# Layer 1's windowed attention on one Trainium2 core: when the exponentials, the division and the gates' loads of a unit are issued

## The chip, the cores and the metric

The kernel runs on one core of one Trainium2 chip. The metric is the device time in microseconds (us) of one launch, median of the runs. Five engines of the core appear in the profile: TensorE (PE, with its weight loads as PEld), VectorE (DVE), ScalarE (ACT), GpSimd (POOL), and SyncE (SP), on whose queue all of this kernel's loads and stores are issued.

## What is computed

One inference step of a two-layer encoder over 2048 prompt frames and 64 sample frames, 1024 wide, in float32. Layer 0 mixes two attentions; the change lies in layer 1, whose attention reads a window of three chunks of 64 frames (its own and two before), with 16 query heads, 2 key heads and a learned sink per head, and whose output is gated and projected:

```python
def _c_layer(h, pos, cache, pre_g, post_g, w_in, sinks, w_out):
    xn = _rms(h, pre_g)
    q, k, v, g = _split(xn @ w_in, C_SIZES)
    ...
    o = _band_prompt(q, k, v, C_PAST_CHUNKS, C_SCALE, sinks=sinks)
    ...
    return h + _rms((o * jax.nn.silu(g)) @ w_out, post_g), state

    s = jnp.einsum('...qhgd,...khd->...hgqk', q, k).astype(jnp.float32) * scale
    s = jnp.where(valid, s, NEG_INF)
    sk = jnp.broadcast_to(sinks.astype(jnp.float32).reshape(hk, g, 1, 1), s.shape[:-1] + (1,))
    p = jax.nn.softmax(jnp.concatenate([s, sk], axis=-1), axis=-1)[..., :-1]
    return jnp.einsum('...hgqk,...khd->...qhgd', p.astype(v.dtype), v)
```

## The kernel before

The kernel runs in five phases. Phase 4 computes layer 1's queries, keys, values and gates (`sQC`, `sKC`, `sVC`, `sGC` in memory), and phase 5, with which the change deals, does layer 1's attention and output projection together. Numbers are kept as a rounded high part and a low part, so that a product of two such numbers is three matmuls (a "triple").

The 2048 frames are 16 blocks of 128, taken in the order 8 to 15, then 0 to 7. A block is four units: chunk `ch` 0 or 1, key head `g` 0 or 1, in the order (0,0), (0,1), (1,0), (1,1). `class Unit` has the stages of a unit:

- `start` (`score`, L1697 to L1701): 8 matmuls give the scores s, 128 rows by 4 x 192 columns; DVE takes the maxima (L1699) and two small results in m (L1700, L1701).
- `exp` (L1708, L1711): ACT computes four exponentials of 128x192 into P, with their sums, and one of the sinks.
- `divide` (L1715 to L1717): DVE adds the sink's term to the sums, takes reciprocals, and multiplies P by them.
- `turn` (L1723): PE transposes P for one part of the window (128 keys, or 64) into t; ACT copies it to PT's high half (L211), and `low` has DVE form the low half (L214).
- `av` (L1730): four matmuls with the values into acc.
- `out` (L1814): ACT copies half of acc to tbm (L211), and DVE adds the halves into the block's output tile OT. After the last unit of a block, the generator `gate` is put into `J.side`.

`gate` loads the gates G (L1735), pauses, multiplies OT by G on POOL (L1738), waits until fewer than two blocks stand between it and the projection, then splits the product into MM: the high half on ACT (L211), the low half on POOL (L1745). The projection multiplies MM by W_out (L964, 16 triples a block); its result z goes through ACT (copy, squares L983), small operations of the inverse root on POOL and DVE (L987, L186 to L197), two multiplications on DVE (L995), and the addition of the residual x on POOL (L1003), and is stored (L1006).

`step(n)` issues one step of a pipeline over the units: the exponentials of unit n+1, the score of unit n+2, unit n's two transposes with `pump(2)` behind each (two triples of the projection), unit n-1's `av` and `out` between them, and at the end unit n+1's division. `J.rest` then moves the gate's generator and the projection's tail by one pause each. The first 8 steps are put in order by a scheduler; for the other 57 the order of PE, DVE, ACT and SP is the order in which the code issues (`manual`), while POOL's is the scheduler's. Every engine takes its instructions in order. OT has two buffers, P three, s two, and G two. A block that would open a third OT (`J.open >= 2`) issues extra `J.rest` and one triple at a time until an older OT is done.

Of the kernel before, what the change touches and what calls it, by code (L numbers as in the profile page):

```python
# [7 lines left out]
F32 = mybir.dt.float32  # L8
# [8 lines left out]
SEQ, DS, PAST, DM = 2048, 64, 1024, 1024  # L17
# [93 lines left out]
def kernel(ctx, tc, a, o, upto=5):  # L111
# [1555 lines left out]
    def phase5():  # L1667

        with ExitStack() as st:
            pool = pools(st, "right")  # L1670
            one, qk, sc, pp, vc = pool("one5", 1), pool("qk5", 2), pool("sc5", 3), pool("pp5", 3), pool("vc5", 2)
            ppt, qp, ot, ev, wo1 = pool("ppt5", 5), pool("qp5", 2), pool("ot5", 2), pool("ev5", 2), pool("woa5", 1)
            ps_s, ps_t = pool("ps_s5", 2, space=PSUM), pool("ps_t5", 2, space=PSUM)
            ps_o, ps_p = pool("ps_o5", 1, space=PSUM), pool("ps_p5", 1, space=PSUM)
            J = jobs([(ps_p, "proj")])
# [53 lines left out]
                for x in range(2):  # L1729
                    nc.tensor.matmul(acc, V, PT[:kk, x], start=(first and x == 0), stop=(last and x == 1))  # L1730

            def gate(OT, t0, r):

                G = qp.tile([128, 8, 128], F32, name="G")
                dma(G[:, :, :r], sGC[:, t0:t0 + r].rearrange("(j p) t -> p j t", p=128))  # L1735
                yield
                yield
                nc.gpsimd.tensor_tensor(OT[:, :, :r], OT[:, :, :r], G[:, :, :r], op=ALU.mult)  # L1738
                while J.made - J.done >= 2 or not J.mm:
                    yield  # L1740
                J.made += 1
                MM = J.mm.tile([128, 2, KT, 128], F32R, name="MM", bufs=2)
                yield
                copy(MM[:, 0, :, :r], OT[:, :, :r])
                nc.gpsimd.tensor_tensor(MM[:, 1, :, :r], OT[:, :, :r], MM[:, 0, :, :r], op=ALU.subtract)  # L1745
                J.open -= r == 128
                for _ in range(DRDY):
                    yield
                J.ready.append((MM, t0, r))
# [25 lines left out]
            class Unit(Soft):  # L1775
# [25 lines left out]
                def out(self):  # L1801
                    B, ch, g = self.B, self.ch, self.g
                    if (ch, g) == (0, 0):
                        while J.open >= 2:
                            J.rest()
                            pump(1)
                        J.open += 1
                        B.OT = ot.tile([128, 8, 128], F32, name="OT", bufs=2)
                    tbm = sc.tile([64, 512], F32, name="tbm", bufs=2)
                    copy(tbm, self.acc[64:128])  # L1810
                    av = self.acc[0:64].rearrange("p (j e q) -> p j e q", e=2, q=64)
                    tv = tbm.rearrange("p (j e q) -> p j e q", e=2, q=64)
                    for e in range(2):
                        nc.vector.tensor_tensor(B.OT[e * 64:e * 64 + 64, g * 4:g * 4 + 4, ch * 64:ch * 64 + 64],  # L1814
                                                av[:, :, e], tv[:, :, e], op=ALU.add)
                    if (ch, g) == (1, 1):
                        J.side.add(gate(B.OT, B.i * 128, 128))

            def sample():
                QS = qp.tile([128, 16, DS], F32R, name="QS", bufs=1)  # L1820
                for x in range(2):
                    dma(f(QS[x * 64:x * 64 + 64]), sQC[x][:, :, SEQ:T].rearrange("h d t -> d h t"))
                KC = qp.tile([128, 2, 2, DS], F32R, name="KS", bufs=1)
                dma(f(KC), sKC[:, :, :, SEQ:T])
                VC = qp.tile([128, 2, 128], F32R, name="VS", bufs=1)
                dma(f(VC[:DS]).rearrange("p g x -> p (g x)"), sVC[SEQ:T])
                OT = ot.tile([128, 8, DS], F32, name="OTs", bufs=1)
                yield
                for g in range(2):
                    u = Soft()  # L1830
                    u.score(lambda c: QS[:, g * 8 + 2 * c:g * 8 + 2 * c + 2].rearrange("p h q -> p (h q)"),
                            [(128, [S.KCS[:, g, x] for x in range(2)]), (64, [KC[:, g, x] for x in range(2)])],
                            192, g)
                    u.exp([0, 1, 2, 3])
                    u.divide()
                    yield
                    PT0, low = u.turn(0, 128)
                    low()
                    PT1, low = u.turn(128, 64)
                    low()  # L1840
                    acc = ps_t.tile([128, 512], F32, name="t")
                    values(acc, PT0, S.VCS[:, g].rearrange("p a d -> p (a d)"), 128, True, False)
                    values(acc, PT1, VC[:64, g], 64, False, True)
                    tbm = sc.tile([64, 512], F32, name="tbm", bufs=2)
                    copy(tbm, acc[64:128])
                    av = acc[0:64].rearrange("p (j e q) -> p j e q", e=2, q=64)
                    tv = tbm.rearrange("p (j e q) -> p j e q", e=2, q=64)
                    for e in range(2):
                        nc.vector.tensor_tensor(OT[e * 64:e * 64 + 64, g * 4:g * 4 + 4], av[:, :, e], tv[:, :, e], op=ALU.add)
                    yield  # L1850
                J.side.add(gate(OT, SEQ, DS))

            units = [(i, ch, g) for i in range(16) for ch in range(2) for g in range(2)]
            blocks = {s: Block(BLOCKS5[s]) for s in range(2)}
# [21 lines left out]
            us = {0: cur, 1: Unit(*units[1])}  # L1876
            us[0].start()
            us[0].exp([0, 1, 2, 3])
            us[0].divide()
            us[1].start()  # L1880
            for _ in range(3):
                wout_tile(W, 1, wo1)
            J.samp.add(sample())

            def step(n):
                cur, prv, nxt = us.get(n), us.get(n - 1), us.get(n + 1)
                if nxt:
                    nxt.exp([0, 1, 2, 3])
                if n + 2 < len(units):
                    us[n + 2] = Unit(*units[n + 2])  # L1890
                    us[n + 2].start()
                    if n % 4 == 1 and n // 4 + 2 < 16:
                        blocks[n // 4 + 2] = Block(BLOCKS5[n // 4 + 2])
                parts = cur.parts() if cur else []
                for b in range(2):
                    low = None
                    if b < len(parts):
                        PT, low = cur.turn(*parts[b][:2])
                        cur.tasks.append(PT)
                    pump(RATE5 / 2)  # L1900
                    if low:
                        low()
                    if b == 0 and prv:
                        prv.av()
                        prv.out()
                if nxt:
                    nxt.divide()
                if prv:
                    us.pop(n - 1)
                    if n % 4 == 0 and n // 4 + 1 in blocks and n > 0:  # L1910
                        blocks[n // 4 + 1].load_values()
                if not J.loaded:
                    J.load.pump(1)
                if n >= NS5:
                    J.samp.pump(1)
                if J.made < FAST5:
                    J.side.pump(SP5)
                J.rest()
# [120 lines left out]
```

## Time and profile before

| | us |
| --- | --- |
| median of 3 runs | 2809.33 |
| lowest and highest run | 2805.70, 2810.07 |
| the profiled execution | 2799.87 |
| its span, first to last instruction | 2798.1 |

The profiled execution lies 9.5 us below the median of the runs; 1.8 us of it are outside the span. All durations below come from this execution. In the views, a line such as `L1717` is a line of the kernel before; a row of instructions gives the start and the length in us, engine, line, operation, the tiles out<-in, shapes, and in brackets how long the engine was idle before it and whose work ended that. A row of a stretch gives start and end, its length, then for each engine the busy us and the instructions in it, and at the end the clock that PE was granted (1.00 is full), the share of the DMA engines, and GB/s.

### The profile page before, as it was taken

What the parts mean: (1) busy time and instruction counts of PE and PEld (TensorE: products, weight loads), DVE (VectorE), ACT (ScalarE), POOL (GpSimd) and SP (SyncE); (2) the same over time, 40 slices, a digit from 0 to 9 for tenths busy, and PEclk for the clock granted to TensorE, in tenths of its full rate; (3) what the DMA queues carried; (4) which work ended last, traced back from release to release, by engine and by line L of the source; (5) the groups of instructions that cost most, each with busy time, mean ns of one, the idle gap of its engine ahead of it and who ended that gap; (6) DMA issues with size and microseconds to landing.
All of it is one profiled execution on the core that took longest, in us unless ns stands there. A gap on an engine that the chain in (4) does not pass through costs nothing.

```text
span 2798.1 us, 46250 instructions
## 1 busy us (share of the span) xinstructions
PE 2593.0 (93%) x16160; PEld 2330.2 (83%) x16160; DVE 1583.9 (57%) x4111; ACT 1360.8 (49%) x3516; POOL 494.3 (18%) x970
## 2 busy tenths in 40 slices
PE   7999999999999999999999998999999987877777
PEld 6999999899988888887778887899999965656565
DVE  5553255442157878777587765752241176666675
ACT  4332233423257777776576665432232165555553
POOL 0001000001013333212003234220010012332223
PEclk9999999999999999999999999999999989998898
DMA  6546444738266666732777766674253574645432
GB/s 235 171 148 203 130 139 158 233 108 253 87 173 172 173 183 185 190 93 84 242 188 206 196 179 182 231 228 142 81 187 97 132 179 94 122 109 107 100 85 68
DMA packets 416760, 438.89 MB, mean 157 GB/s; under 512 B 116224, under 2 KB 343368, under 8 KB 413296
## 3 DMA queue, kind: packets, MB, share of 16 engines
q1 hardware_dynamic: 416528, 435.93, 54.4%
q8 instruction: 129, 2.11, 0.3%
q14 instruction: 103, 0.84, 0.1%
HBM read 283.78 MB, written 157.09 MB: 158 GB/s over the span
## 4 chain that ended last, share of the span: by engine, by line
PE 72%; DVE 13%; ACT 6%; DMA 5%; issue 2%; POOL 1%; SPq 0%; ACTq 0%; DVEq 0%; POOLq 0%
PE pm L237 36%; PE proj L964 9%; PE s L683 5%; PE acc L754 4%; PE t L726 3%; DVE PT L214 3%; PE acc L1228 2%; DVE P L1717 2%; PE acc L1730 2%; PE s L1176 2%; PE t L1203 2%; PE t L1723 2%; DVE OT L1814 2%; ACT tbm L211 1%; DVE m L689 1%
## 5 line engine op out<-in xcount | busy, mean ns | idle before, releaser
L237 PE MATMUL pm<-X,W 128*128 128x384 f32 (+2 forms) x4536 | 753.9, 325 | 2.6 <-DVE ev L214 1.3
L237 PEld LDWEIGHTS pm<-X,W 128*128 128x128 f32 x4536 | 731.6, 189 | 6.1 <-ACT X L211 1.8
L211 ACT ACTIVATE PT<-t 128x512 fp32r<-128x512 f32 (+3 forms) x704 | 344.8, 503 | 293.0 <-PE t L1723 97.8
L214 DVE SCALAR_TENSOR_TENSOR PT<-t,PT 128x512 fp32r<-128x512 f32 (+4 forms) x688 | 378.8, 569 | 80.6 <-ACT PT L211 77.5
L964 PE MATMUL proj<-Wo,MM 128*128 128x512 f32 (+1 forms) x1416 | 415.2, 426 | 3.5 <-ACT z L211 3.1
L964 PEld LDWEIGHTS proj<-Wo,MM 128*128 128x128 f32 (+1 forms) x1416 | 260.0, 197 | 59.9 <-issue 7.8
L214 DVE SCALAR_TENSOR_TENSOR ev<-pm,ev 128x256 fp32r<-128x256 f32 (+3 forms) x197 | 98.6, 503 | 333.5 <-ACT ev L430 97.4
L237 PE MATMUL pm<-W,X 128*128 128x256 f32 (+5 forms) x2040 | 281.1, 297 | 0.0
L237 PEld LDWEIGHTS pm<-W,X 128*128 128x128 f32 (+1 forms) x2040 | 272.0, 187 | 1.1
L702 ACT ACTIVATE P<-s,m 128x512 f32<-128x512 f32 (+9 forms) x344 | 209.5, 616 | 33.1 <-DVE m L691 30.5
L683 PE MATMUL s<-KA,Q 128*128 128x512 f32 (+7 forms) x640 | 201.2, 396 | 9.3 <-ACT P L702 8.4
L228 DVE TENSOR_TENSOR W<-R,W 128x768 fp32r<-128x768 f32 (+3 forms) x114 | 116.3, 1055 | 134.3 <-ACT W L227 133.9
L726 PE MATMUL t<-ident,P 128*128 128x128 f32 x1088 | 176.3, 276 | 3.5 <-ACT P L702 0.8
L689 DVE TENSOR_REDUCE m<-s 128x1 f32<-128x480 f32 (+7 forms) x216 | 132.4, 613 | 79.9 <-PE s L683 79.4
L1723 PE MATMUL t<-ident,P 128*128 128x128 f32 (+1 forms) x512 | 87.2, 298 | 96.0 <-DVE P L1717 92.5
L726 PEld LDWEIGHTS t<-ident,P 128*128 128x128 f32 x1088 | 134.5, 141 | 41.9 <-ACT P L702 15.1
L754 PE MATMUL acc<-PT,V 128*128 128x256 f32 x1152 | 156.0, 285 | 6.3 <-DVE OT L763 6.3
L1723 PEld LDWEIGHTS t<-ident,P 128*128 128x128 f32 (+1 forms) x512 | 55.9, 135 | 124.6 <-issue 91.5
L211 ACT ACTIVATE tbm<-acc 64x512 f32<-64x512 f32 (+1 forms) x136 | 77.5, 570 | 154.7 <-PE acc L1730 124.5
L754 PEld LDWEIGHTS acc<-PT,V 128*128 128x128 f32 x1152 | 140.4, 188 | 11.5 <-PE t L726 6.0
L1814 DVE TENSOR_TENSOR OT<-acc,tbm 64x256 f32<-64x256 f32 x128 | 53.3, 416 | 122.7 <-ACT tbm L211 92.5
L683 PE MATMUL s<-KR,Q 128*128 128x384 f32 (+6 forms) x320 | 116.3, 363 | 1.7 <-DMA Q<-sQR 1.7
(238 smaller groups left out, 3994.1 us busy)
## 6 DMA issues: line engine op xcount, KB each, us to landing
Q<-sQA SPq DMA_DIRECT2D x128, 128.0 KB, 3.1
sWO<-W SPq DMA_DIRECT2D x32, 512.0 KB, 3.8
Q<-sQB SPq DMA_DIRECT2D x128, 128.0 KB, 3.4
Wo<-sWO SPq DMA_DIRECT2D x16, 1024.0 KB, 8.6
Q<-sQC SPq DMA_DIRECT2D x64, 256.0 KB, 6.5
R<-in_ab_w_in_dram SPq DMA_DIRECT2D x40, 384.0 KB, 4.0
K<-sKB SPq DMA_DIRECT2D x56, 256.0 KB, 5.6
V<-sVB SPq DMA_DIRECT2D x24, 512.0 KB, 6.5
```

Of the source, the lines that this page charges most:

```text
L211: nc.scalar.activation(out, in_, AF.Copy)
L214: nc.vector.scalar_tensor_tensor(out, x, scale, hi, op0=ALU.mult, op1=ALU.subtract)
L228: nc.vector.tensor_tensor(Wv[:, 1, k0:k1], Rv, Wv[:, 0, k0:k1], op=ALU.subtract)
L237: nc.tensor.matmul(ps, lhs(x, k), rhs(y, k), start=(j == 0), stop=(j == n - 1))
L683: nc.tensor.matmul(s[:r, :n], self.Q[:, x, self.qo:self.qo + r], rhs, start=(x == 0), stop=(x == 2))
L689: nc.vector.tensor_reduce(m[:r, j:j + 1], s[:r, :n], axis=AX.X, op=ALU.max)
L702: nc.scalar.activation(self.P[:r, o0:o0 + n], self.s.pop(j)[:r, :n], AF.Exp, bias=self.m[:r, 6:7], accum_out=acc)
L726: nc.tensor.transpose(t[:, b], self.P[:, (b0 + b) * 128:(b0 + b + 1) * 128], ident)
L754: nc.tensor.matmul(acc[:, (i // 2) % 2], H.V[:, b0 + b], PT[:, x, b], start=(b0 + b == 0 and x == 0), stop=(b0 + b == i and x == 1))
L964: nc.tensor.matmul(p, M[:, x, k, :r], W[k][:, y, cs], start=(k == k0 and t == 0), stop=(k == k1 - 1 and t == 2))
L1723: nc.tensor.transpose(t[:kk, c * 128:c * 128 + 128], self.P[:, c, k0:k0 + kk], ident)
L1814: nc.vector.tensor_tensor(B.OT[e * 64:e * 64 + 64, g * 4:g * 4 + 4, ch * 64:ch * 64 + 64], av[:, :, e], tv[:, :, e], op=ALU.add)
```

## The change

Exponentials: step n now ends with the exponentials of unit n+2, whose score stands at the step's beginning; before, step n began with those of unit n+1. Division: unit n+1 is divided in the middle of step n, after unit n-1's `av` and before its `out`; before, at the end of the step. For the first two units, the exponentials of unit 1 are issued before the steps begin. Gates: the load of G is taken out of `gate` into the new function `gates`, called in `out` of the third unit of a block, (1,0), and `gate` has one pause less. Output tiles: OT has three buffers, and a block waits at three open ones.

```diff
-            def gate(OT, t0, r):
-
+            def gates(t0, r):
                 G = qp.tile([128, 8, 128], F32, name="G")
                 dma(G[:, :, :r], sGC[:, t0:t0 + r].rearrange("(j p) t -> p j t", p=128))
-                yield
+                return G
+
+            def gate(OT, G, t0, r):
+
                 yield
                 nc.gpsimd.tensor_tensor(OT[:, :, :r], OT[:, :, :r], G[:, :, :r], op=ALU.mult)
...
-                        while J.open >= 2:
+                        while J.open >= 3:
                             J.rest()
                             pump(1)
                         J.open += 1
-                        B.OT = ot.tile([128, 8, 128], F32, name="OT", bufs=2)
+                        B.OT = ot.tile([128, 8, 128], F32, name="OT", bufs=3)
+                    if (ch, g) == (1, 0):
+                        B.G = gates(B.i * 128, 128)
...
-                        J.side.add(gate(B.OT, B.i * 128, 128))
+                        J.side.add(gate(B.OT, B.G, B.i * 128, 128))
...
-                J.side.add(gate(OT, SEQ, DS))
+                J.side.add(gate(OT, gates(SEQ, DS), SEQ, DS))
...
             us[0].start()
             us[0].exp([0, 1, 2, 3])
+            us[1].start()
             us[0].divide()
-            us[1].start()
+            us[1].exp([0, 1, 2, 3])
...
                 cur, prv, nxt = us.get(n), us.get(n - 1), us.get(n + 1)
-                if nxt:
-                    nxt.exp([0, 1, 2, 3])
                 if n + 2 < len(units):
-                    us[n + 2] = Unit(*units[n + 2])
-                    us[n + 2].start()
+                    ahead = us[n + 2] = Unit(*units[n + 2])
+                    ahead.start()
+                else:
+                    ahead = None
+                if n + 2 < len(units):
                     if n % 4 == 1 and n // 4 + 2 < 16:
                         blocks[n // 4 + 2] = Block(BLOCKS5[n // 4 + 2])
...
                     if b == 0 and prv:
                         prv.av()
+                    if b == 0 and nxt:
+                        nxt.divide()
+                    if b == 0 and prv:
                         prv.out()
-                if nxt:
-                    nxt.divide()
+                if ahead:
+                    ahead.exp([0, 1, 2, 3])
```

In the built program, DVE's stream over one step (the score's maxima of unit n+2 come first; the numbers behind the names tell one buffer's use from the next) stood like this before:

```order
L1699 TENSOR_REDUCE m_29342<-s_29341 128x4
L1700 SCALAR_TENSOR_TENSOR m_29342<-m_29342,nssink_25805 128x4
L1701 TENSOR_TENSOR m_29342<-m_29342,ssink_25804 128x4
L214 SCALAR_TENSOR_TENSOR PT_29359<-t_29354,PT_29359 128x512
L1814 TENSOR_TENSOR OT_29168<-acc_29368,tbm_29373 64x4x64 x2
L214 SCALAR_TENSOR_TENSOR PT_29382<-t_29377,PT_29382 64x512
L1715 TENSOR_TENSOR m_29255<-m_29255 128x4
L1716 RECIPROCAL m_29255<-m_29255 128x4
L1717 TENSOR_TENSOR P_29335<-P_29335,m_29255 128x768
```

The same step of the changed program, whose lines from 1738 on have moved by two to nine:

```order
L1699 TENSOR_REDUCE m_29358<-s_29357 128x4
L1700 SCALAR_TENSOR_TENSOR m_29358<-m_29358,nssink_25805 128x4
L1701 TENSOR_TENSOR m_29358<-m_29358,ssink_25804 128x4
L214 SCALAR_TENSOR_TENSOR PT_29375<-t_29370,PT_29375 128x512
L1715 TENSOR_TENSOR m_29297<-m_29297 128x4
L1716 RECIPROCAL m_29297<-m_29297 128x4
L1717 TENSOR_TENSOR P_29349<-P_29349,m_29297 128x768
L1818 TENSOR_TENSOR OT_29182<-acc_29389,tbm_29397 64x4x64 x2
L214 SCALAR_TENSOR_TENSOR PT_29406<-t_29401,PT_29406 64x512
L995 SCALAR_TENSOR_TENSOR z_28962<-z_28962,rs_29230,g_post_21588 128x512
```

The three rows of the division have moved up from the end, over the second PT half and the OT addition.

ACT's stream at the same place, before (s and m number 29254 and 29255 are unit n+1's, 29341 and 29342 unit n+2's):

```order
L1708 ACTIVATE P_29335,m_29255<-s_29254,m_29255 128x192 x4
L1711 ACTIVATE m_29255<-m_29255 128x4
L211 ACTIVATE PT_29359<-t_29354 128x512
L211 ACTIVATE tbm_29373<-acc_29368 64x512
L211 ACTIVATE PT_29382<-t_29377 64x512
L211 ACTIVATE z_29295<-proj_29298 128x512
L1708 ACTIVATE P_29398,m_29342<-s_29341,m_29342 128x192 x4
```

And after (s 29296 is unit n+1's, 29357 unit n+2's):

```order
L211 ACTIVATE z_29248<-proj_29251 128x512
L1708 ACTIVATE P_29349,m_29297<-s_29296,m_29297 128x192 x4
L1711 ACTIVATE m_29297<-m_29297 128x4
L211 ACTIVATE MM_29295<-OT_28896 128x1024
L211 ACTIVATE PT_29375<-t_29370 128x512
L983 ACTIVATE sq_29250,ss2_29249<-z_29248 128x512
L211 ACTIVATE tbm_29397<-acc_29389 64x512
L211 ACTIVATE PT_29406<-t_29401 64x512
L1708 ACTIVATE P_29415,m_29358<-s_29357,m_29358 128x192 x4
```

In both streams a unit's exponentials stand behind the last PT copy and z of one step and ahead of the first PT copy of the next, and they are those of the unit that DVE divides in that next step (m 29255 before, m 29297 after): against these neighbours they have not moved. What has moved is the copy into MM: it now stands behind the exponentials and ahead of the PT copy, while before it stood, in another step of the block, behind the squares.

SP's stream over one block, before (x is the residual's load, out_0 the result's store, VC and VH the values, KC and Q the keys and queries):

```order
L1033 DMA x_28721<-sH_71 128x1024
L1769 DMA VC_28820<-sVC_73 128x2x256
L1773 DMA VH_28822<-sVC_73 64x256
L1758 DMA KC_28845<-sKC_72 128x4x256
L1763 DMA Q_28847<-sQC0_74 64x16x64
L1763 DMA Q_28847<-sQC1_75 64x16x64
L1735 DMA G_28960<-sGC_76 128x8x128
L1006 DMA out_0_dram<-x_28447 128x1024
```

After:

```order
L1033 DMA x_28674<-sH_71 128x1024
L1734 DMA G_28759<-sGC_76 128x8x128
L1771 DMA VC_28849<-sVC_73 128x2x256
L1775 DMA VH_28851<-sVC_73 64x256
L1760 DMA KC_28867<-sKC_72 128x4x256
L1765 DMA Q_28869<-sQC0_74 64x16x64
L1765 DMA Q_28869<-sQC1_75 64x16x64
L1006 DMA out_0_dram<-x_28410 128x1024
```

G has moved up, ahead of the values, keys and queries of the blocks to come (each Q pair is issued twice; it is shown once).

## The prediction

> **What bounds the kernel now.** I began with the page's busy line, its clock row, and the costliest groups, looking for an engine that is nearly full and for what it still waits for.
>
> ```profile
> PE 2593.0 (93%) x16160; PEld 2330.2 (83%) x16160; DVE 1583.9 (57%) x4111; ACT 1360.8 (49%) x3516; POOL 494.3 (18%) x970
> PEclk9999999999999999999999999999999989998898
> ...
> L1723 PE MATMUL t<-ident,P 128*128 128x128 f32 (+1 forms) x512 | 87.2, 298 | 96.0 <-DVE P L1717 92.5
> ```
>
> TensorE (PE) is busy 93% of the time, and its largest wait is in layer 1's attention: the transposes of the softmax weights P (L1723) stood idle 96.0 us, 92.5 of it until VectorE (DVE) had divided P (L1717). The clock row dips in the same last fifth of the span. The view of stretches cuts this part into the opening, the steps 9 to 62 (from the first transpose of unit 9 to that of unit 63), and the end.
>
> ```profile
> core 0: us, PE busy (x) PEld busy (x) DVE busy (x) ACT busy (x) POOL busy (x), PEclk, DMA share, GB/s
> 2232.15:2314.36 82.21, 71.50 (x370) 54.73 (x368) 55.18 (x123) 46.79 (x159) 7.32 (x4) 0.85 0.69 177
> 2314.36:2748.49 434.13, 340.21 (x1673) 258.97 (x1674) 288.75 (x585) 225.90 (x727) 129.62 (x222) 0.92 0.47 100
> ```
>
> The 54 steps take 434.13 us: 8.04 a step, 32.2 for a block of four units (13.5 blocks). PE idles 434.13 - 340.21 = 93.9 us, and its clock averages 0.92, so of its 340.21 busy us some 0.08 x 340 = 27 are half-rate time that full rate would not need (an estimate). What is left is 313 us, 23.2 a block. The waits in this stretch, and the instructions of one block on PE:
>
> ```profile
> PE t L1723 <- DVE P L1717: 89.0, 52, 4.3
> POOL OT L1738 <- DMA G<-sGC: 46.0, 10, 6.2
> DVE OT L1814 <- POOL MM L1745: 29.3, 11, 3.3
> ...
> 2600.58 2.34 PE L964 MATMUL proj<-Wo,MM 128*128 128x512 f32 x9
> 2608.48 0.63 PE L1723 MATMUL t<-ident,P 128*128 128x128 f32 x4 [0.84 <-DVE P L1717]
> 2616.74 1.09 PE L1723 MATMUL t<-ident,P 128*128 128x128 f32 x4 [3.69 <-DVE P L1717]
> 2617.48 4.19 PE L964 MATMUL proj<-Wo,MM 128*128 128x512 f32 x9
> 2633.74 0.63 PE L1723 MATMUL t<-ident,P 128*128 128x128 f32 x4 [1.52 <-DVE P L1717]
> ...
> 2616.70:2622.70 6.00, 5.96 (x16) 4.47 (x17) 1.99 (x6) 1.21 (x3) 2.27 (x12) 0.50 0.46 145
> ```
>
> PE waits for P in every step: 0.8 us, 1.5 us, and once a block about 4. Behind the long wait the clock stands at 0.50 for 6 us, and nine output-projection matmuls take 4.19 us instead of 2.34. The long wait comes from here:
>
> ```profile
> 2612.28 0.85 DVE L1814 TENSOR_TENSOR OT<-acc,tbm 64x256 f32<-64x256 f32 x2 [1.43 <-ACT tbm L211]
> 2613.14 0.68 DVE L214 SCALAR_TENSOR_TENSOR PT<-t,PT 64x512 fp32r<-64x512 f32 x1
> 2613.75 1.63 DVE L1715 TENSOR_TENSOR m<-m 128x4 f32<-128x4 f32 x1
> ...
> 2610.68 2.38 POOL L1738 TENSOR_TENSOR OT<-OT,G 128x1024 f32<-128x1024 f32 x1 [5.20 <-DMA G<-sGC]
> 2613.03 2.34 POOL L1003 TENSOR_TENSOR x<-z,x 128x1024 f32<-128x1024 f32 x1
> ```
>
> The division's first operation, 0.14 us elsewhere, took 1.63 us and ended at 2615.38, just where GpSimd's (POOL's) two large operations ended (2615.37). The OT addition and PT's low half, which each read PSUM, ran in the same time at their usual length. So a POOL operation can hold up a DVE operation whose inputs are both in SBUF.
>
> **The change part by part.** *Exponentials and division.* Moving the exponentials from the head of step n+1 to the end of step n leaves ACT's stream as it is: in both programs they follow the second PT copy and z, and precede the next step's first PT copy. So this part alone I count at nothing; no engine's work moves past it but the copy into MM, below. The division does move, on DVE: from the end of step n, where the transposes that need it follow after one score (about 1 us), to mid-step, ahead of OT and the second PT half, both of which wait for PE and ACT of that step. The instructions are the same in number. The wait for P, the last to end in nearly every step, should go: 93.9 us at most, and 27 us of slow clock with it. What is late next is DVE. Its step, from the starts of the rows below:
>
> ```profile
> 2597.21 0.85 DVE L1814 TENSOR_TENSOR OT<-acc,tbm 64x256 f32<-64x256 f32 x2 [1.82 <-ACT tbm L211]
> 2598.09 0.68 DVE L214 SCALAR_TENSOR_TENSOR PT<-t,PT 64x512 fp32r<-64x512 f32 x1
> 2598.70 0.14 DVE L1715 TENSOR_TENSOR m<-m 128x4 f32<-128x4 f32 x1
> 2599.09 0.96 DVE L1717 TENSOR_TENSOR P<-P,m 128x768 f32<-128x768 f32 x1
> 2599.97 0.95 DVE L1699 TENSOR_REDUCE m<-s 128x4 f32<-128x768 f32 x1
> 2601.49 0.69 DVE L214 SCALAR_TENSOR_TENSOR PT<-t,PT 128x512 fp32r<-128x512 f32 x1 [0.18 <-ACT PT L211]
> 2602.09 0.74 DVE L995 SCALAR_TENSOR_TENSOR z<-z,rs,g_post 128x512 f32<-128x512 f32 x1
> ```
>
> OT 0.88, PT 0.61, division 1.27, maximum with its two small operations 1.3 (1.52 less the 0.18 wait), PT 0.6: 4.7 a step, and with two z operations (0.7 each) and the root's two (0.4) 20.6 a block, against PE's 23.2. That fits, with 2.6 us to spare. But POOL's three large operations of a block hold 2.4 us each, 7.1 in all, and some 8 us of DVE's 20.6 (the divisions, the small operations on m, z) have both inputs in SBUF. I follow a block by hand. ScalarE's (ACT's) part:
>
> ```profile
> 2597.89 0.60 ACT L211 ACTIVATE z<-proj 128x512 f32<-128x512 f32 x1
> 2598.39 0.41 ACT L1708 ACTIVATE P<-s,m 128x192 f32<-128x192 f32 x1
> 2599.97 0.22 ACT L1711 ACTIVATE m<-m 128x4 f32<-128x4 f32 x1
> 2635.51 1.05 ACT L211 ACTIVATE MM<-OT 128x1024 fp32r<-128x1024 f32 x1
> 2636.64 2.37 POOL L1745 TENSOR_TENSOR MM<-OT,MM 128x1024 fp32r<-128x1024 f32 x1 [13.35 <-ACT MM L211]
> ...
> 2619.65 0.15 DVE L187 TENSOR_SCALAR rs<-rs 128x1 int32<-128x1 int32 x1 [1.80 <-POOL rs L186]
> ```
>
> PE's steps alternate: five projection triples (0.73 us each: nine matmuls 2.18 from start to start) or three, so 6.5 and 5.1 us. Take zero at the long step in which MM is copied. ACT first has z, the exponentials (1.8) and MM, so POOL's low half of MM holds 3.5 to 5.9; the division, due at 4.6, runs 5.9 to 7.1, OT to 8.0, PT to 8.6. The gate's product starts as OT ends and holds 8.0 to 10.4, so z waits from 8.6 and ends at 11.1. In the short step (from 6.5) DVE runs through maximum, PT, division (done 14.4), OT, PT and z by 16.5; the next step's transposes (due 12.5) wait 1.9 us. The residual sum on POOL then holds 16.5 to 18.9: the small operations on m wait, and behind them the root, whose POOL part comes after that sum; the division ends at 21.9, and transposes due at 20.9 wait 1.0. In the fourth step DVE catches up. **2.9 us of waits stay of 9.0 a block** (7.0 idle, 2.0 clock); I take 3.0. Below is 0, if these lock-outs fall into DVE's idle time; above is 9, if nothing is won. Neither wait is over 2 us, and no row with so short a wait shows the slow clock:
>
> ```profile
> 2709.70 0.63 PE L1723 MATMUL t<-ident,P 128*128 128x128 f32 x4 [2.01 <-DVE P L1717]
> 2709.00:2714.00 5.00, 4.30 (x25) 3.33 (x26) 4.91 (x8) 1.69 (x3) 2.40 (x1) 1.00 0.11 43
> ```
>
> The Trainium skill, SBUF — State Buffer, "Who interferes with whom", speaks against dividing in mid-step: a DVE instruction with two SBUF inputs and a GpSimd instruction that reads SBUF exclude each other, and the one that starts first keeps the port for its whole length, however long. By that rule every lock-out of this walk holds in full and 3.0 stands; without it the 20.6 us would fit and the waits be near nothing. The 1.63 us row agrees with it.
>
> *Gates, output tiles.* The G load moves on SP from behind the next Q loads to before them, and the gate's product loses one step of delay. POOL's 46.0 us behind G and DVE's 29.3 behind the old OT tile go, but neither engine is last there, so I count nothing; were they on the path, their part is already inside the 93.9. What G is moved past has room:
>
> ```profile
> 2599.30 5.07 SPq L1763 DMA_DIRECT2D Q<-sQC  x4
> 2604.41 1.33 SPq L1735 DMA_DIRECT2D G<-sGC  x1
> ```
>
> Q is wanted five steps after its issue, 5 x 6.5 = 32 us; 5.07 of issue and 1.33 more change nothing. At a 26 us block the DMA share rises from 0.47 to 0.58. If that cover went, a late Q would cost its lateness once a block.
>
> *Opening.* Unit 2's exponentials come ahead of the sample's, so a score that waited for a slot need not:
>
> ```profile
> 2260.38 2.02 PE L1697 MATMUL s<-KC,Q 128*128 128x192 f32 x8 [3.40 <-ACT P L1708]
> ```
>
> I take 4 us (the wait and a little clock; from 12, with the slow stretch behind it, down to -8 if the new order is worse). *End:* four projection triples move from behind the last unit into the steps; PE's sum is unchanged: 0.
>
> **Sum.** 93.9 + 27.2 - 13.5 x 3.0 + 4 = 85 us. The profiled execution took 2799.87, so 2715; the timed runs have a median of 2809.33, 9 us more, and on that footing it is 2724.
>
> **The rivals.** *PE becomes the bound* (chance 0.20): the lock-outs fall into DVE's 2.6 us of spare time; 0.75 us a block stays: 2809 - (121 - 10 + 4) = 2694. For it: the OT addition, the PT halves and the maximum, most of DVE's step, run beside POOL. Against: the spare 2.6 us is less than the 7.1 that POOL holds. *DVE becomes the bound* (0.22): POOL's operations meet a division more often than in my walk, and PE loses 6 us a block: 2809 - (121 - 81 + 4) = 2765. For it: DVE with its waits inside was busy 288.75 us, 21.4 a block, and all must fit into less. *Slower* (0.05): a wait of some 2.4 us in each of four steps, behind a division held by POOL, long enough to halve the clock each time (2.0 us, the 27 us over 13.5 blocks with one long wait each): 17.6 us against 9.0 removed, 13.5 x 8.6 = 116, less the opening's 4: 2921. It decides as soon as waits and clock pass 9.3 us a block. For it: a row with 2.19 us of wait does show slow matmuls:
>
> ```profile
> 2393.63 0.69 PE L1723 MATMUL t<-ident,P 128*128 128x128 f32 x4 [2.19 <-DVE P L1717]
> 2394.01 3.89 PE L964 MATMUL proj<-Wo,MM 128*128 128x512 f32 x9
> ```
>
> Against: POOL has three such operations a block, and they leave DVE a step to recover. *No change* (0.03): the division, though issued earlier, still ends last because DVE is late by as much as today: 2809.
>
> **How the numbers follow.** My forecast, 1.8 to 4.5 us of waits a block, has 0.50 and gives 2708 to 2745; the likeliest time is 2724. The range 2688 to 2775 leaves out the bottom of PE's case (0.03), the upper part of DVE's (0.09) and the last two (0.08). Faster by over 0.2% (about 6 us, what a measurement of this kernel can tell): 0.50 + 0.20 + 0.22 = 0.92; same 0.03; slower 0.05.
>
> **What would show it.** The wait of t for P should fall from 89 us to under 45, with no wait over 2.2 us as a rule, clock near 1.00, and four steps in about 26 us. DVE's small operations on m and z should show lengths of 1 to 2.4 us that end with a POOL operation: if they don't, PE's case is right. POOL should no longer wait for G, nor OT for MM. I am wrong if PE's waits turn up at acc or at the projections, or if the slow clock stays.

## The result, and the profile after

The changed kernel takes 2702.99 us (median of 4 runs, 2701.31 to 2706.91), the kernel before, timed beside it, 2807.51 us: a ratio of 0.9633, 95% interval 0.9613 to 0.9654. The profiled execution took 2703.56 us with a span of 2701.8 us, 96.3 us less than the profiled one of before.

The page of the changed kernel: span, busy time and, in 40 slices, the granted clock of PE in tenths.

```profile
span 2701.8 us, 46285 instructions
PE 2564.7 (95%) x16160; PEld 2311.6 (86%) x16160; DVE 1602.8 (59%) x4111; ACT 1359.8 (50%) x3516; POOL 502.5 (19%) x970
PEclk9999999999999999999899999999999998999999
```

Busy time by stretch of the changed kernel (us, then PE, PEld, DVE, ACT, POOL busy, granted clock, DMA share, GB/s): from the opening to unit 9's first transposes, the 54 steps from there to unit 63's, and the end.

```profile
2225.00:2314.34 89.34, 80.02 (x440) 63.43 (x440) 55.23 (x124) 47.38 (x160) 8.97 (x5) 0.87 0.77 192
2314.34:2656.26 341.92, 313.22 (x1691) 241.68 (x1689) 308.84 (x585) 226.63 (x732) 138.49 (x230) 1.00 0.56 125
2656.26:2701.80 45.54, 34.01 (x146) 25.92 (x145) 25.00 (x60) 12.10 (x24) 13.81 (x12) 0.92 0.28 92
```

The same 54 steps took 434.13 us before. PE's idle time in them fell from 93.9 to 28.7 us (341.92 - 313.22), and its busy time by 27.0, with the clock at 1.00 instead of 0.92 and 18 matmuls more in the stretch. Waits of the changed kernel in these steps (us in all, times, longest):

```profile
POOL x L1003 <- DVE z L995: 69.6, 12, 5.9
POOL OT L1740 <- DVE OT L1818: 41.7, 14, 15.4
PE t L1723 <- DVE P L1717: 28.7, 25, 2.5
```

PE still waits for P and for nothing else that counts. POOL waits for DVE now (and, as before, for ACT's copy into MM), no longer for G. One block on PE, then the three places on DVE and POOL that hold it up (start, length, and in brackets the idle time before, with its releaser):

```profile
2564.74 0.63 PE L1723 MATMUL t<-ident,P 128*128 128x128 f32 x4
2571.66 0.63 PE L1723 MATMUL t<-ident,P 128*128 128x128 f32 x4 [1.67 <-DVE P L1717]
2572.04 2.34 PE L964 MATMUL proj<-Wo,MM 128*128 128x512 f32 x9
2578.94 0.63 PE L1723 MATMUL t<-ident,P 128*128 128x128 f32 x4 [0.61 <-DVE P L1717]
...
2562.02 1.36 DVE L1715 TENSOR_TENSOR m<-m 128x4 f32<-128x4 f32 x1
2565.99 2.38 DVE L995 SCALAR_TENSOR_TENSOR z<-z,rs,g_post 128x512 f32<-128x512 f32 x1
2574.54 1.57 DVE L1700 SCALAR_TENSOR_TENSOR m<-m,nssink 128x4 f32<-128x4 f32 x1
...
2560.97 2.38 POOL L1747 TENSOR_TENSOR MM<-OT,MM 128x1024 fp32r<-128x1024 f32 x1 [6.01 <-ACT MM L211]
2565.43 2.39 POOL L1740 TENSOR_TENSOR OT<-OT,G 128x1024 f32<-128x1024 f32 x1 [2.07 <-DVE OT L1818]
2573.72 2.37 POOL L1003 TENSOR_TENSOR x<-z,x 128x1024 f32<-128x1024 f32 x1 [5.90 <-DVE z L995]
```

Read each DVE row against the POOL row over the same time. The division's first operation ends at 2563.38, MM's low half at 2563.35. z starts 0.56 us after the gate's product, which ends at 2567.82; z ends 0.55 us later, having taken 2.38 us for 0.73 us of work. The small operation on m ends at 2576.11, the residual sum at 2576.09. The 1.67 us wait follows z, the 0.61 us wait follows m, and the nine matmuls behind the longer wait run at full clock (2.34 us).

### The profile page after: what moved, and what is told of

It reads as the page before. It is cut to its first block, busy times and chain, and to the rows that moved or that the text cites. A ratio compares the mean times of both kernels' runs of the same rounds, so it can differ in the third digit from the quotient of the medians.

```text
span 2701.8 us, 46285 instructions
## 1 busy us (share of the span) xinstructions
PE 2564.7 (95%) x16160; PEld 2311.6 (86%) x16160; DVE 1602.8 (59%) x4111; ACT 1359.8 (50%) x3516; POOL 502.5 (19%) x970
## 4 chain that ended last, share of the span: by engine, by line
PE 72%; DVE 14%; ACT 6%; DMA 4%; issue 2%; POOL 1%; SPq 0%; ACTq 0%; DVEq 0%; POOLq 0%
PE pm L237 38%; PE proj L964 8%; PE s L683 6%; PE acc L754 4%; DVE PT L214 3%; PE t L726 3%; PE acc L1228 3%; PE s L1176 2%; PE t L1203 2%; DVE z L995 1%; DVE P L1717 1%; ACT P L702 1%; DVE m L689 1%; POOL x L1003 1%; PE t L1723 1%
## 5 line engine op out<-in xcount | busy, mean ns | idle before, releaser
L964 PE MATMUL proj<-Wo,MM 128*128 128x512 f32 (+1 forms) x1440 | 401.3, 408 | 5.6 <-ACT z L211 4.6
L964 PEld LDWEIGHTS proj<-Wo,MM 128*128 128x128 f32 (+1 forms) x1440 | 249.4, 187 | 55.6 <-ACT z L211 8.8
L689 DVE TENSOR_REDUCE m<-s 128x1 f32<-128x480 f32 (+7 forms) x216 | 132.4, 613 | 80.6 <-PE s L683 80.3
L754 PE MATMUL acc<-PT,V 128*128 128x256 f32 x1152 | 156.0, 285 | 6.6 <-DVE OT L763 6.6
L1228 PE MATMUL acc<-PT,V 128*128 128x256 f32 x672 | 111.5, 298 | 6.5 <-DVE OT L1238 4.3
L1180 DVE CUSTOM_DVE_ANT_0 s<-s,bias 128x640 f32<-128x640 f32 (+4 forms) x128 | 95.2, 744 | 35.0 <-PE s L1176 33.5
L227 ACT ACTIVATE W<-R 128x768 fp32r<-128x768 f32 (+3 forms) x114 | 98.2, 909 | 29.6 <-DMA R<-in_ab_w_in_dram 13.0
```

What stands on the lines that cost most here:

```text
L227: nc.scalar.activation(Wv[:, 0, k0:k1], Rv, AF.Copy)
L689: nc.vector.tensor_reduce(m[:r, j:j + 1], s[:r, :n], axis=AX.X, op=ALU.max)
L754: nc.tensor.matmul(acc[:, (i // 2) % 2], H.V[:, b0 + b], PT[:, x, b], start=(b0 + b == 0 and x == 0), stop=(b0 + b == i and x == 1))
L964: nc.tensor.matmul(p, M[:, x, k, :r], W[k][:, y, cs], start=(k == k0 and t == 0), stop=(k == k1 - 1 and t == 2))
L1228: nc.tensor.matmul(acc, self.H.V[:, self.base - self.H.b0 + b], self.PT[:, x, off + b], start=(b == 0 and x == 0), stop=(b == nblk - 1 and ...
```

## Experiments

Theory: the division's place in DVE's order is the gain, and what is left is DVE held out by POOL. The rivals at the start: exponentials or gates and tiles carry a good part. In the table "opening" runs from the first matmul of line 1588 to unit 9, "steps" are the same 54 steps in each kernel, "idle" is that stretch less PE's busy time in it, "clock" is the granted clock there, and "end" is what follows the steps, all but the clock in us of the profiled run. The ratio is to the kernel before, timed beside each.

| kernel | median | ratio, 95% interval | opening | steps | idle | clock | end |
|---|---|---|---|---|---|---|---|
| before | 2807.51 | 1 | 82.2 | 434.1 | 93.9 | 0.92 | 49.6 |
| changed | 2702.99 | 0.9633 (0.9613 to 0.9654) | 80.8 | 341.9 | 28.7 | 1.00 | 45.5 |
| division only | 2731.52 | 0.9738 (0.9709 to 0.9766) | 88.6 | 363.0 | 37.6 | 0.94 | 49.5 |
| exponentials only | 2797.85 | 0.9974 (0.9957 to 0.9990) | 78.9 | 428.9 | 90.9 | 0.92 | 49.6 |
| gates, tiles only | 2781.09 | 0.9908 (0.9875 to 0.9941) | 88.2 | 411.0 | 84.4 | 0.97 | 45.5 |
| division, exponentials | 2724.26 | 0.9715 (0.9682 to 0.9747) | 83.7 | 353.2 | 34.6 | 0.96 | 50.8 |
| changed, two tiles | 2705.56 | 0.9642 (0.9627 to 0.9657) | 77.4 | 341.2 | 29.5 | 1.00 | 45.5 |
| changed, one pause more | 2720.72 | 0.9704 (0.9684 to 0.9723) | 77.8 | 346.1 | 30.7 | 0.93 | 61.7 |
| changed, 1/8 product | 2686.89 | 0.9577 (0.9563 to 0.9591) | 82.9 | 320.6 | 9.6 | 1.00 | 45.6 |
| changed, halves | 2684.08 | 0.9563 (0.9541 to 0.9585) | 80.8 | 320.7 | 11.4 | 1.00 | 45.5 |
| changed, quarters | 2675.34 | 0.9551 (0.9530 to 0.9572) | 77.4 | 312.8 | 4.1 | 1.00 | 45.5 |
| changed, product in halves | 2691.24 | 0.9596 (0.9581 to 0.9610) | 84.4 | 328.7 | 17.0 | 1.00 | 45.5 |
| div., exp., halves | 2697.36 | 0.9610 (0.9594 to 0.9626) | 80.3 | 330.0 | 18.4 | 0.98 | 48.0 |
| before, halves | 2797.20 | 0.9978 (0.9964 to 0.9993) | 84.7 | 427.0 | 93.5 | 0.94 | 49.6 |

The opening differs by 3.4 us between the changed kernel and the one with two tiles, whose steps are alike, so differences of that size in it say nothing.

### The change in its parts

**Division only.** The kernel before with one move:

```diff
                     if b == 0 and prv:
                         prv.av()
+                    if b == 0 and nxt:
+                        nxt.divide()
+                    if b == 0 and prv:
                         prv.out()
-                if nxt:
-                    nxt.divide()
```

> Only the division is moved, from the end of the step to its middle; exponentials, gates and output tiles as before. My theory: the division's place in DVE's order is the whole gain, so the time is that of the changed kernel or little more: 2703 to 2717, the upper end if a division now has to wait for exponentials that stand behind ACT's copy of MM (1.05 us, once in each of 13.5 blocks). Rival A, exponentials two steps ahead are what makes the early division possible: the division waits for them in the middle of each step, PE loses some 2 us a step, 2780 to 2850. Rival B, gates and the third output tile bring a third of the gain: about 2740.

2731.52 us: 73 us below the 2804.87 of before that was timed beside it, by far the largest part, but 14.5 us above the expected range, between it and rival B's 2740, and not rival A's. Part of what is missing is in the steps, 21.1 us. Waits and the window of this kernel's steps:

```profile
PE t L1723 <- DVE P L1717: 33.7, 13, 4.2
...
2322.50:2685.48 362.98, 325.41 (x1675) 251.23 (x1674) 315.09 (x583) 224.09 (x730) 141.81 (x222) 0.94 0.56 119
```

PE waits 13 times, not 25, but for up to 4.2 us, and the slow clock is still there (0.94). The end is 4 us longer too; that the opening is 7.8 us longer stays unexplained.

**Exponentials only.** The kernel before with `ahead.exp` at the end of a step, the division behind it:

```diff
-                if nxt:
-                    nxt.exp([0, 1, 2, 3])
...
+                if ahead:
+                    ahead.exp([0, 1, 2, 3])
                 if nxt:
                     nxt.divide()
```

> Only the exponentials are issued earlier (two steps ahead); the division stays at the end of the step, gates and output tiles as before. My theory: ACT's order hardly changes and DVE still comes to the division last, so no change: 2800 to 2812, and PE's wait for P stays near 89 us. Rival A: if the exponentials held the division back, half of the gain or more appears: 2750 or less.

2797.85 us: 7.0 us less than before, just under my range, and nothing like rival A's half. PE's wait for P is 89.2 us in this kernel's steps, against 89.0:

```profile
PE t L1723 <- DVE P L1717: 89.2, 53, 4.3
```

**Gates and tiles only.** The kernel before with the gate's and the tile's part of the diff.

> Only the gate's load is issued earlier and there are three output tiles; the softmax in its old order. My theory: POOL's 46 us behind G and DVE's 29 us behind the old output tile go, but neither engine is last, so 2800 to 2812. Rival B: what DVE waits for its output tile delays the divisions behind it, so up to 29 us come off: 2775 to 2795.

2781.09 us, 23.8 us less: in rival B's range. The part that I had counted at nothing is worth a quarter of the gain. Load, pause and tile were not taken apart in the old order, so whether it is by rival B's way, the wait for the tile, stays open. The waits and the window of its steps:

```profile
PE t L1723 <- DVE P L1717: 82.1, 52, 2.6
...
2323.45:2734.45 411.00, 326.59 (x1688) 249.37 (x1689) 314.36 (x587) 226.17 (x729) 141.77 (x235) 0.97 0.47 104
```

As many waits as before (52), but the longest is 2.6 us instead of 4.3. Of the 23.1 us that the steps lost, 13.6 are PE's busy time (340.2 to 326.6): slow clock that no longer follows long waits.

**Division and exponentials, old gates.** The changed kernel with the gate's and the tile's part undone.

> Exponentials and division as in the changed kernel, but gates and output tiles as before (the load in the gate's own job, two tiles). My theory: 2700 to 2708, as the changed kernel. Rival B: with steps of 6.5 us instead of 8 the old output tile comes later against DVE's order, and the waits of the addition push the division behind it: 2715 to 2745.

2724.26 us: rival B's range again, 21.3 us above the changed kernel, but not by its way: DVE waits for the old tile once, 2.3 us. The parts hardly touch each other: alone they bring 73.4 (division), 7.0 (exponentials) and 23.8 (gates), 104.2 together, and the changed kernel lies 104.5 below the kernel before. What the old gates do is seen in one long step of this kernel, on PE, DVE and POOL, with a window over the slow matmuls:

```profile
2589.11 1.09 PE L1723 MATMUL t<-ident,P 128*128 128x128 f32 x4 [4.11 <-DVE P L1717]
2589.84 4.19 PE L964 MATMUL proj<-Wo,MM 128*128 128x512 f32 x9
...
2571.90 0.85 DVE L1814 TENSOR_TENSOR OT<-acc,tbm 64x256 f32<-64x256 f32 x2 [0.35 <-ACT tbm L211]
2577.30 2.88 DVE L995 SCALAR_TENSOR_TENSOR z<-z,rs,g_post 128x512 f32<-128x512 f32 x1
2583.22 1.59 DVE L1700 SCALAR_TENSOR_TENSOR m<-m,nssink 128x4 f32<-128x4 f32 x1
2585.53 2.23 DVE L1715 TENSOR_TENSOR m<-m 128x4 f32<-128x4 f32 x1
...
2577.01 2.62 POOL L1745 TENSOR_TENSOR MM<-OT,MM 128x1024 fp32r<-128x1024 f32 x1 [9.98 <-ACT MM L211]
2582.40 2.38 POOL L1003 TENSOR_TENSOR x<-z,x 128x1024 f32<-128x1024 f32 x1 [2.77 <-DVE z L995]
2585.39 2.34 POOL L1738 TENSOR_TENSOR OT<-OT,G 128x1024 f32<-128x1024 f32 x1 [0.61 <-DMA G<-sGC]
...
2589.00:2594.00 5.00, 4.89 (x14) 4.07 (x15) 4.48 (x12) 1.21 (x3) 1.61 (x7) 0.50 0.29 98
```

MM's low half has held z for 2.1 us in the step before. POOL is free at 2584.78 and starts the gate's product when G lands, at 2585.39, 0.14 us before the division's first operation. The division, already 1.4 us late from the residual sum, loses another 2.1; PE waits 4.11 us and runs nine matmuls in 4.19 us at a clock of 0.50. In the changed kernel G is there, the product starts as soon as OT's last addition ends, one step ahead of the sum, and MM's low half comes ahead of the product: no operation is late twice.

### What the gates' part consists of

**Two tiles.** The changed kernel with `J.open >= 2` and `bufs=2`.

> The changed kernel with two output tiles in place of three; the gate's load stays early. The run with the new softmax and the old gates lost 21 us. Theory G, the load is what counts, because it sets when POOL's gate product starts and so which of DVE's operations it holds up: 2698 to 2710, as the changed kernel. Rival T, the third tile is what counts: 2718 to 2728.

2705.56 us, within the changed kernel's interval: the third tile brings nothing here that can be measured. (In the old order, where DVE waited 29.3 us for the old tile, it was not tried alone.)

**One pause more.** One `yield` more ahead of the product, so that the generator has as many pauses as before the change, with G loaded early:

```diff
             def gate(OT, G, t0, r):
 
                 yield
+                yield
                 nc.gpsimd.tensor_tensor(OT[:, :, :r], OT[:, :, :r], G[:, :, :r], op=ALU.mult)
```

> The changed kernel, load early and three tiles, but the gate's product is issued one step later. POOL then has the gate's product beside the residual sum, 2.4 us each, in one step. Theory G: DVE's small operations on m are held for up to 4.8 us, PE waits about 4 us in some steps, the slow clock comes back there, 2715 to 2735. Rival: the product's place is without effect, only the wait for the load was: 2698 to 2710.

2720.72 us, within the range, and POOL waits for G only once in the steps (4.8 us). But the way is not as I wrote it: what moved is not the product. POOL, DVE and PE of this kernel:

```profile
2559.73 2.40 POOL L1741 TENSOR_TENSOR OT<-OT,G 128x1024 f32<-128x1024 f32 x1 [5.68 <-DVE OT L1819]
2563.91 2.62 POOL L1748 TENSOR_TENSOR MM<-OT,MM 128x1024 fp32r<-128x1024 f32 x1 [1.79 <-ACT MM L211]
2569.30 2.37 POOL L1003 TENSOR_TENSOR x<-z,x 128x1024 f32<-128x1024 f32 x1 [2.76 <-DVE z L995]
...
2558.80 0.85 DVE L1819 TENSOR_TENSOR OT<-acc,tbm 64x256 f32<-64x256 f32 x2 [0.35 <-ACT tbm L211]
2564.20 2.88 DVE L995 SCALAR_TENSOR_TENSOR z<-z,rs,g_post 128x512 f32<-128x512 f32 x1
2570.12 1.58 DVE L1700 SCALAR_TENSOR_TENSOR m<-m,nssink 128x4 f32<-128x4 f32 x1
...
2573.92 0.73 PE L1723 MATMUL t<-ident,P 128*128 128x128 f32 x4 [2.02 <-DVE P L1717]
2574.30 3.90 PE L964 MATMUL proj<-Wo,MM 128*128 128x512 f32 x9
```

The product still starts 0.1 us after OT's last addition (it ends at 2559.65), as in the changed kernel. What comes later is MM's low half, behind the product and no longer ahead of it, and with it the projection. Starts of POOL's three operations in the blocks shown, in us from the end of OT's last addition (the product of this kernel stands at 0.1 in 11 of 12 blocks of the steps):

| kernel | MM's low half | product | residual sum | median |
|---|---|---|---|---|
| changed | -4.4 | 0.1 | 8.4 | 2702.99 |
| changed, one pause more | 4.3 | 0.1 | 9.7 | 2720.72 |
| division, exponentials | 4.3 | 12.6 | 9.7 | 2724.26 |

So with the old number of pauses the early load, with the third tile, moves the product by 12.5 us and the median by 3.5 us, with intervals that overlap. The pause that goes brings 17.7 us. Whether it would bring them with G loaded late was not run.

POOL's three operations stand within 12 us here and hold DVE in two steps that follow each other. The longest wait is 3.1 us, not 4, and PE's idle time is only 2 us more than in the changed kernel (30.7 against 28.7). What costs is the clock, 0.93: behind a 2.02 us wait the nine matmuls took 3.90 us instead of 2.34. (The projection falls behind by more than a block's 48 matmuls: 62 more stand in the end, 208 against 146, which is 16.2 us longer.)

### The lock-outs

**An eighth of the product.**

```diff
-                nc.gpsimd.tensor_tensor(OT[:, :, :r], OT[:, :, :r], G[:, :, :r], op=ALU.mult)
+                nc.gpsimd.tensor_tensor(OT[:, 0:1, :r], OT[:, 0:1, :r], G[:, 0:1, :r], op=ALU.mult)
```

> The changed kernel with only an eighth of the gate's product computed (seven eighths of the gating are left out), so that POOL holds DVE out for 0.3 us and not 2.4. Theory of the lock-outs: the first of z's two operations takes 0.7 us and not 2.4, and PE's 1.65 us wait in that step goes, 13 x 1.65 = 21 us: 2680 to 2690. Rival, DVE has simply too much to do in these steps: 2698 to 2706.

This kernel leaves out seven eighths of the gating. 2686.89 us, as the lock-outs say: 16.1 us less. The product's 13 operations took 0.46 us each, z's two 0.73 us (once 1.40), and PE's idle time in the steps fell by 19.1 us. So DVE has time enough for its work. The eighth also runs earlier, since it needs OT's first part only, so hold and place are both changed here. The operations on z in this kernel (count, then least, median and longest in ns):

```profile
L995 DVE SCALAR_TENSOR_TENSOR z<-z,rs,g_post x26: 731/734/1403, 2348.9 to 2634.5; 128x512 f32<-128x512 f32 x24, 64x512 f32<-64x512 f32 x2
```

**Halves.** Nothing left out; each of the three POOL operations in two pieces:

```diff
-                nc.gpsimd.tensor_tensor(OT[:, :, :r], OT[:, :, :r], G[:, :, :r], op=ALU.mult)
+                for j in (slice(0, 4), slice(4, 8)):
+                    nc.gpsimd.tensor_tensor(OT[:, j, :r], OT[:, j, :r], G[:, j, :r], op=ALU.mult)
```

and in the same way MM's low half, and the residual sum by 512 columns.

> The changed kernel with POOL's three large operations of a block each issued as two halves (1.2 us and 1.2 us). Theory of the lock-outs: if DVE's waiting operation gets in between the halves, z comes 1.2 us earlier, the division and the maximum's small operations up to 1.2: 1 to 1.6 us of the 2.3 us a block go, 2682 to 2692. Rival: the second half starts before DVE's operation does, and nothing changes: 2700 to 2708.

2684.08 us, within the range, 18.9 us below the changed kernel. DVE and POOL of this kernel (its lines stand one to three lower down):

```profile
2547.88 0.26 DVE L1716 TENSOR_TENSOR m<-m 128x4 f32<-128x4 f32 x1
2548.38 1.80 DVE L1718 TENSOR_TENSOR P<-P,m 128x768 f32<-128x768 f32 x1
2551.58 1.29 DVE L995 SCALAR_TENSOR_TENSOR z<-z,rs,g_post 128x512 f32<-128x512 f32 x1
...
2544.74 1.29 POOL L1742 TENSOR_TENSOR OT<-OT,G 128x512 f32<-128x512 f32 x1 [4.20 <-PE t L1724]
2546.83 2.53 POOL L1750 TENSOR_TENSOR MM<-OT,MM 128x512 fp32r<-128x512 f32 x2 [0.79 <-ACT MM L211]
2551.02 1.30 POOL L1742 TENSOR_TENSOR OT<-OT,G 128x512 f32<-128x512 f32 x1 [1.66 <-DVE OT L1821]
```

Two things happen. MM's two pieces follow each other without a gap, and the division's first operation still ends at 2548.14, about when the first piece does: it came in between, and the second piece holds only the division's last operation, 1.80 us instead of 0.96. And the product's first half no longer waits for OT's last addition, since it needs half of OT only; it runs six microseconds ahead of the second, with MM's pieces of the block before in between. z is held 0.56 us (1.29 for 0.73) instead of 1.65.

**Quarters.** As the halves, in four pieces each.

> As the run in halves, but each of POOL's three large operations in four pieces of 0.6 to 0.7 us. PE waited only 9.9 us for P in the steps of that run (0.6 us a block), so little is left. Theory of the lock-outs: the holds get shorter still and at most those 9.9 us go: 2674 to 2685. Rival, more pieces meet DVE's operations more often: 2686 to 2700.

2675.34 us, the fastest kernel here, 27.7 us below the changed one. Waits and the window of its steps:

```profile
PE t L1724 <- DVE P L1718: 3.1, 6, 1.1
...
2313.82:2626.66 312.84, 308.76 (x1690) 239.89 (x1689) 281.55 (x585) 225.16 (x732) 170.76 (x347) 1.00 0.62 137
```

PE is idle 4.1 us of 312.84. POOL pays for it with 32 us more of busy time (170.76 against 138.49), which costs nothing there. In these steps PE is now the bound.

**The product alone in halves.**

> The changed kernel with only the gate's product in two halves; MM's low half and the residual sum whole. Theory: the product is what holds z and makes the 1.65 us wait, so most of the gain of the run in halves is here, as in the run with an eighth of it: 2683 to 2692. Rival, the three operations bring a third each: 2694 to 2700.

2691.24 us: 11.8 us less, at the upper end of the range. Of the 18.9 us that the halves bring, 11.8 are the product's; MM and the sum share the other 7.

**Division, exponentials and old gates, in halves.**

> New softmax order, old gates and two tiles, and POOL's three operations in halves. Theory G: the old gates cost 21 us because the gate's product, started by G's arrival, falls beside the residual sum and the two hold DVE out for 4.8 us and PE goes to the slow clock; in halves these holds are short and the gates' part shrinks: 2684 to 2698. Rival, the wait for G itself costs: 21 us above the run in halves, 2702 to 2710.

2697.36 us, at the edge of the range: the gates' part is 13.3 us (to 2684.08), where it was 21.3 with whole operations. Shorter holds make the places of POOL's operations matter less, as theory G has it, but not little: the clock in its steps is 0.98. With two tiles and late MM, DVE also waits for the old tile here (16.7 us, 12 times), so not all of the 13.3 us need be holds.

**Before, in halves.**

> The kernel before, its division still at the end of the step, with POOL's three operations in halves. If the lock-outs lengthen the old waits too (a division of 2.9 us where it takes 1.0, waits of up to 4.3 us with the slow clock behind them): 2765 to 2795. Rival, the old order is bound by the division's place alone, and lock-outs fall into DVE's idle time: 2800 to 2812.

2797.20 us, 7.1 us less and just below the rival's range; the other theory had 2765 to 2795. Waits and the window of its steps:

```profile
PE t L1724 <- DVE P L1718: 88.7, 52, 4.3
...
2323.37:2750.41 427.04, 333.50 (x1673) 253.83 (x1674) 279.06 (x585) 225.66 (x727) 136.56 (x262) 0.94 0.48 102
```

PE's wait for P stays at 88.7 us, so in the old order the division's place is the bound. The same edit that brings 18.9 us in the new order brings 7.1 in the old.

## Why the prediction was right, and where not

**The mechanism held.** The wait of t for P fell from 89.0 to 28.7 us (I had said under 45), the steps' clock went to 1.00, four steps take 25.3 us (341.92 / 13.5; I had said about 26). POOL's wait for G is gone. The division alone, with no other edit, brings 73 us.

**Three lock-outs, where the walk put them.** The walk had MM's low half delaying the division by 1.3 us (1.2 shown: 1.36 for 0.14), the gate's product delaying z by 1.8 (1.65 shown), the residual sum delaying the small operations on m. Its two waits, 1.9 and 1.0 us, measured 1.67 and 0.61: **2.3 us a block, not 3.0**. In the stretch as a whole 28.7 us of idle time stayed, not 40.5, the largest difference of size: 11.8 us.

**The step that failed: gates and tiles at nothing.** I wrote that neither engine is last, so POOL's 46.0 us behind G count nothing. The third tile is indeed worth nothing in the changed kernel, but the part as a whole is worth 21 us. POOL's wait by itself cost little: without it, but with the old pauses, the time is 2720.72 us, against 2724.26 with it. What I priced at nothing without a reason is the pause that `gate` loses. With it gone MM's low half stands ahead of the product, the three operations of the block shown spread over 15 us instead of 12, all waits of PE but one are at most 1.70 us, and the clock stays full: 17.7 us. The rows of that chain were in the prediction: the product there starts on G, runs into the residual sum, and both end with the division's first operation, behind which PE waits longest. I read from them that POOL can hold DVE, and did not ask what moves POOL's operations. The walk, though, had MM's low half ahead of the product, which is true only with the pause gone, and started the product "as OT ends", which is true only with G loaded early. So its sum held for the whole change while its parts did not; a walk with the three operations where they used to stand would have met sum and product together.

**Exponentials at nothing.** 7.0 us without the division moved, outside its interval (0.9957 to 0.9990), and 7.3 us with it, where the two kernels' intervals overlap: small. I had seen that ACT's copy into MM goes behind them (1.08 us) and gave it no price. That the copy is the cause was not tried.

**The smaller terms.** The opening's 4 us did not come: it went from 82.2 to 80.8 us, and the earlier phases took 1.4 us longer. The 3.4 us score wait did not go; it moved to the sample's second score, with the slow clock behind it. The opening of the changed kernel on PE, and a window over what follows:

```profile
2262.99 0.69 PE L1697 MATMUL s<-KCS,QS 128*128 128x128 f32 x2 [3.29 <-ACT P L1708]
...
2262.00:2278.00 16.00, 14.45 (x58) 12.06 (x58) 11.76 (x25) 8.89 (x37) 0.00 (x0) 0.51 0.94 231
```

The end, counted at nothing, lost 4.1 us: with MM copied earlier 14 matmuls fewer are left for it (146 against 160); the kernels with the old gates still have 160. The slow clock's 27 us went in full.

**The rivals.** PE as the bound is not the changed kernel but the one in quarters, 2675 us. DVE as the bound, in the sense of POOL meeting it more often, is what the old gates and the old pauses show (2724 and 2721 us). **The sum.** Between the profiled executions 65.2 us of idle time in the steps, 27.0 of PE's busy time there and 4.1 at the end make 96.3, against 85. The rest of the distance from 2724 to 2703 is the footing: I had added the 9 us by which the profiled execution of before lay under its median, and that of the changed kernel lies at its median.

## What to carry to other kernels

An engine that is not last still decides by the start of its instructions whom it shuts out. So price a change on such an engine by what its instructions then run into, not only by whether it ends last; here one pause less was worth 17.7 us though POOL was busy for about 40% of the steps. When a run is to move one operation, look in its trace at which one moved: the pause left the product where it was. Where a long POOL operation stands beside DVE operations with both inputs in SBUF, cut it into pieces: that is one loop each, and brought 19 us in halves and 28 in quarters, but only after the larger bound, the division's place, had gone (7 us in halves before that). And check that a hand walk and the price of its parts rest on the same start times.

## What the runs showed of the hardware

The slow clock does not follow from the length of the wait alone. Waits of t with nine output-projection matmuls right behind, in the steps of the 14 profiles: of 76 waits of 1.50 to 1.70 us, 75 were followed by full speed (2.33 to 2.36 us) and one, of 1.56 us, by 3.54 us; of 40 waits of 1.72 to 2.6 us, 23 were followed by slow matmuls; of 30 over 3.0 us, 29 (and one of two in between). Of 55 shorter ones, two (0.25 and 1.48 us). The exception of 1.56 us, in the kernel with division, exponentials and halves; six matmuls ahead of it still ran at full speed (1.63 us):

```profile
2470.58 1.63 PE L964 MATMUL proj<-Wo,MM 128*128 128x512 f32 x6
2475.50 1.11 PE L1724 MATMUL t<-ident,P 128*128 128x128 f32 x4 [1.56 <-DVE P L1718]
2476.26 3.54 PE L964 MATMUL proj<-Wo,MM 128*128 128x512 f32 x9
```

The Trainium skill, TensorE: Matmul & The Clock Gate, "HAM oscillation — how this bites in real kernels", asks for no idle gaps of TensorE over about 3.4 us. Here the slow clock followed waits of about two microseconds in about half of the cases, so the measurement decides; what else counts, short idle times around the wait perhaps, was not tried.

A DVE operation gets in between two POOL pieces that follow each other without a gap: in 12 of 13 blocks of the kernel in halves the division's first operation ended with MM's first piece (2548.14 in the block shown), while the second ran on (to 2549.36). The rows of before did not show that. The Trainium skill, SBUF — State Buffer, "Who interferes with whom", has the port held for the length of an instruction; the halves agree (z 2.38 us beside a whole product, 1.29 beside a half).
